# Adaptive layer-norm sums of a Conformer/mLSTM block: half the step rate over the q products, the rest over the wk products, and another PSUM bank

## The chip, the cores and the metric

The kernel runs on one core of a Trainium2 chip. The metric is the device time of one execution in microseconds (us), lower is better. The kernel before takes 1817.89 us, the median of three runs (1816.94 to 1818.36). A change of this kernel of less than about 0.2% (3.6 us) cannot be told from no change.

Five engines work side by side, each through its own list of instructions in the order of the list: TensorE (PE in the profile; its weight loads are listed as PEld), VectorE (DVE), ScalarE (ACT), GpSimd (POOL) and SyncE (SP). SP issues nearly all the loads from memory here, also in the order of its list. An instruction that waits holds up everything behind it on its engine.

## The reference

The block is two layers over 256 latent tokens (model width 1024) with 256 context tokens ahead of them. Layer 0 mixes tokens by a convolution, layer 1 by a bidirectional mLSTM with 4 heads of width 512; each is followed by an MLP with squared ReLU. All is float32. Each sub-layer is modulated by six vectors, which a matrix product of the conditioning vector gives:

```
def adaln(cvec, w, b):
    return jnp.split(jax.nn.silu(cvec) @ w + b, 6, axis=-1)
...
for i in range(DEPTH):
    sh1, sc1, g1, sh2, sc2, g2 = adaln(c[:, None, :], ada_w[i], ada_b[i])
    csh1, csc1, cg1, csh2, csc2, cg2 = adaln(c_ctx, ada_w[i], ada_b[i])
    u = modulate(h, sh1, sc1)
    ...
    h = layer_norm(ALPHA * h + g1 * y, ln1_g[i], ln1_b[i])
    h = layer_norm(ALPHA * h + g2 * sq_relu_mlp(modulate(h, sh2, sc2), ...), ...)
```

`ada_w[i]` is a 1024 x 6144 matrix, and there are only two rows to multiply with it: `c` and `c_ctx`. In the mLSTM the queries are `xc @ w_q` and the keys `xc @ w_k`. The kernel does not make the keys for the scores; it multiplies the queries with `w_k` first and then with `xc`.

## The kernel before

**Matrix products.** Every float32 operand is split into a high and a low part (`wh` and `wl` for weights), and one product is three matmuls (lines 177, 180 and 181). Weights come in 1 MB loads into a tile `raw` (line 150, three buffers); ACT casts 128x1024 of it to `wh` (line 154), DVE subtracts to get `wl` (line 155), with four buffers each. Results go to PSUM banks: a kind `mm` with three banks, `ln` with two, `cv` with two and `fl` with one. `psum()` without a name takes the next `mm` bank.

**adaLN of layer 1.** Part of this product is not done by TensorE. The class `AdaV` does it in steps: a step loads 128x512 of `ada_w` into a tile `ar` (line 353; one buffer, so the next load waits until DVE has read this one) and DVE multiplies it with one column of `c` and `c_ctx` and adds to two accumulators `L` (line 357 for the first step of eight, line 359 for the other seven). After eight steps the accumulators hold, for 512 outputs, one partial sum per partition. `rows` adds these over the partitions by two matmuls with a matrix of ones (line 372) into a PSUM bank, and ACT copies the result to a tile `F` (line 374). After two such halves (one in the last unit) `end` transposes `F` by four matmuls (line 381), and DVE adds the bias (line 382).

There are five units of this in two lists. `ada_n1` runs inside the MLP of layer 0, one step per block of 128 outputs. `ada_n2` has three units, 40 steps: 16 steps run during the last half of the v product, and the other 24 in what follows. Its steps are called by the loops of the other products:

- `queries(h)` makes the queries of head `h`: eight pieces of 24 matmuls (128x256), each with 128x1024 of `wq`, and one step after each piece.
- `pair(p)` makes the queries of two heads, then runs over the 16 row blocks `m` of `wk`: for each, 24 matmuls of 128x272 (12 per head) into `mm` banks, the split of the result into `rr`, and 12 matmuls of 128x512 into four score accumulators, which are the two `ln` banks, one `cv` bank and the `fl` bank.

Pair 0 (heads 0 and 1) therefore takes 16 steps in its two `queries`, the whole second unit, and pair 1 eight steps in the first of its two, the third unit.

**What sets the order.** The program is written in the order above, and a scheduler then sets each engine's list by its own estimates. It may put an instruction later or earlier than written, as long as the data allow it; on the chip the list is fixed. Buffers are given by turn: a tile that takes the next `mm` bank shifts the bank of all `mm` tiles behind it, and must wait for the bank's last reader.

Of the kernel before, what the change touches and what calls it, by code (L numbers as in the profile page):

```python
# [21 lines left out]
C = 256  # L22
# [50 lines left out]
def hybrid_kernel(ctx: ExitStack, tc: tile.TileContext, xT, vecs_d, wdw_d, ada0_w, ada_w, wg_d, pw1a, pw1, pw2, w1_0, w2_0,  # L73
# [12 lines left out]
    def nm(s):  # L86
        uid[0] += 1
        return f"{s}_{uid[0]}"
# [3 lines left out]
    def tmp(tag, dt=F32):  # L92
        return tp.tile([P, T], dt, tag=tag, name=nm(tag), bufs={"E": 4, "S": 2, "L": 2, "F": 1}[tag])
# [8 lines left out]
    def psum(tag="mm"):  # L102
        return pp.tile([P, 512], F32, tag=tag, name=nm(tag), bufs={"mm": 3, "ln": 2, "fl": 1, "cv": 2}[tag])
# [44 lines left out]
    def raw_load(src):  # L148
        raw = wp.tile([P, 2048], F32, tag="raw", name=nm("raw"), bufs=3)
        nc.sync.dma_start(raw[:, :src.shape[-1]], src)  # L150
        return raw
# [8 lines left out]
    def split_w(src, make=None):  # L160
        n = src.shape[-1]
        if make is not None:
            his, los = [], []
            for i in range(0, n, T):
                his.append(make(F32R))
                los.append(make(F32R))
                split(his[-1], los[-1], src[:, i:i + T])
            return his, los
        hi = wp.tile([P, 1024], F32R, tag="wh", name=nm("wh"), bufs=NW)[:, :n]
        lo = wp.tile([P, 1024], F32R, tag="wl", name=nm("wl"), bufs=NW)[:, :n]  # L170
        anchors.append(split(hi, lo, src))
        return hi, lo
# [3 lines left out]
    def mm3(ps, wh, wl, xh, xl, start, stop):  # L176
        a = nc.tensor.matmul(ps, wh, xh, start=start, stop=False)  # L177
        if pin[0]:
            tc.keep_in_program_order(a)
        nc.tensor.matmul(ps, wh, xl, start=False, stop=False)  # L180
        nc.tensor.matmul(ps, wl, xh, start=False, stop=stop)  # L181

    def kcol(w, kt):
        if isinstance(w[0], list):
            w, kt = (w[0][kt // 4], w[1][kt // 4]), kt % 4
        return w[0][:, kt * P:(kt + 1) * P], w[1][:, kt * P:(kt + 1) * P]
# [5 lines left out]
    def gemm_steps(w_ap, groups, rhs, n, epi, ko=0, pre=None):  # L192


        if isinstance(rhs, dict):
            parts = [(LO, rhs[0]), (HI, rhs[1])]
        else:
            parts = [(slice(0, n), rhs)]
        kh_n = len(parts[0][1]) // 8
        groups = list(groups)  # L200
        pre = pre or {}
        raws = {}
        if ko:
            ws, pss = [], []
            for m in range(ko):
                g = groups[m // 2]
                if m not in pre:
                    if g not in raws:
                        raws[g] = raw_load(w_ap[g, 0])
                    pre[m] = split_w(raws[g][:, (m % 2) * 1024:(m % 2 + 1) * 1024])  # L210
                ws.append(pre[m])
                pss.append(psum("mm" if m < 3 else "cv")[:, :n])
            for kt in range(8):
                for m in range(ko):
                    mm3(pss[m], *kcol(ws[m], kt), *rhs[kt], kt == 0, kt == 7)
            for m in range(ko):
                epi(m, pss[m])
        for gi, g in enumerate(groups):
            if 2 * gi + 1 < ko:
                continue  # L220
            ms = [m for m in (0, 1) if 2 * gi + m >= ko]
            pss = {m: psum()[:, :n] for m in ms}
            for kh in range(kh_n):
                raw = raws.get(g)
                for m in ms:
                    w = pre.get((g, kh, m))
                    if w is None:
                        if raw is None:
                            raw = raw_load(w_ap[g, kh])
                        w = split_w(raw[:, m * 1024:(m + 1) * 1024])  # L230
                    for sl, r in parts:
                        for kt in range(8):
                            mm3(pss[m][:, sl], *kcol(w, kt), *r[kh * 8 + kt], kh == 0 and kt == 0,
                                kh == kh_n - 1 and kt == 7)
                    if kh == kh_n - 1:
                        epi(gi * 2 + m, pss[m])
                    yield
# [103 lines left out]
    class AdaV:  # L341
# [22 lines left out]
                self.end()  # L364

        def rows(self, n):
            ps = psum("fl")
            if n == 0:
                self.sb = tmp("F")
            for s in range(2):  # L370
                j = 32 * (2 * n + s)
                nc.tensor.matmul(ps[j:j + 32, :], ones[:, 0:32], self.acc[s], start=True, stop=True,  # L372
                                 tile_position=(0, j))
            nc.scalar.copy(self.sb[64 * n:64 * n + 64], ps[64 * n:64 * n + 64])

        def end(self):
            nu, o = self.nu, _OFF[f"ada_b{self.l}"][0] + 4 * self.u0
            r = 64 * nu
            tr = psum("fl")[:, 0:4 * r]
            for b in range(4):  # L380
                nc.tensor.transpose(tr[:, b * r:(b + 1) * r], self.sb[:r, b * P:(b + 1) * P], ident[:r, :r])
            nc.vector.tensor_tensor(
                ada[self.l][:, 4 * self.u0:4 * (self.u0 + nu), :].rearrange("p (v b) s -> p b v s", b=4),
                tr.rearrange("p (b v s r) -> p b v s r", b=4, v=nu, s=2)[:, :, :, :, 0],
                vecs[:, o:o + 4 * nu].rearrange("p (v b o) -> p b v o", b=4, o=1).broadcast_to([P, 4, nu, 2]), op=ALU.add)
# [302 lines left out]
    for h_ in range(2):  # L688
        wd = F()[:NTAP, :]
        nc.sync.dma_start(wd, wdw_d[0:NTAP, h_ * 512:(h_ + 1) * 512])  # L690
        for t, w_ in ((Hc, WC), (Hs, WS)):
            ps = psum("ln")
# [253 lines left out]
    ada_g2, ada_n1, ada_n2 = Ada(0, 10, 2), AdaVs(1, 0, 4), AdaVs(1, 4, 8 - Z.fill)  # L946
# [131 lines left out]
    def flush():  # L1078
        while late:
            late.pop(0)()  # L1080
# [26 lines left out]
    preq = {(0, 0, m): split_w(rx[:, m * 1024:(m + 1) * 1024]) for m in (0, 1)}  # L1107
# [5 lines left out]
    xcl = [(h_[:, HI], l_[:, HI]) for h_, l_ in xcs]  # L1113
# [5 lines left out]
    def queries(h):  # L1119
        qq = []  # L1120

        def q_epi(m, ps):
            if m < 2:
                flush()
            t = qd.tile([P, 2, QW], F32R, tag="qq", name=nm("qq"), bufs=8)
            split(t[:, 0, :C], t[:, 1, :C], ps)
            split(t[:, 0, C:], t[:, 1, C:], rk[:, 4 * h + m, :])
            qq.append((t[:, 0, :], t[:, 1, :]))

        for _ in gemm_steps(wq, range(2 * h, 2 * h + 2), xcl, C, q_epi, pre=preq):  # L1130
            ada_n2.step()
        return qq

    def pair(p):
        qq = [queries(2 * p + i) for i in range(2)]
        flush()
        acc = [psum(t) for t in ("ln", "ln", "cv", "fl")]
        todo = []

        def scores(n):  # L1140
            while len(todo) > n:
                m, r = todo.pop(0)
                for b in range(4):
                    mm3(acc[b], xcs[m][0][:, b * P:(b + 1) * P], xcs[m][1][:, b * P:(b + 1) * P], *r, m == 0, m == ET - 1)

        def end():
            scores(0)
            for b in range(4):
                t = X()
                nc.scalar.mul(t, acc[b], DH ** -0.5)  # L1150
                for i in range(2):
                    S[2 * p + i, b] = t[:, i * C:(i + 1) * C]

        for m in range(ET):
            if m % 2 == 0:
                raw = raw_load(wk[p, m // 2])
                ws = [split_w(raw[:, i * 1024:(i + 1) * 1024]) for i in range(2)]
            r = RR(F32R), RR(F32R)
            for i in range(2):
                ps = psum()[:, :QW]  # L1160
                for kt in range(4):
                    mm3(ps, *kcol(ws[i], m % 2 * 4 + kt), *qq[i][kt], kt == 0, kt == 3)
                split(r[0][:, i * C:(i + 1) * C], r[1][:, i * C:(i + 1) * C], ps[:, :C])
                nc.vector.tensor_tensor(wgp[1][:, m, 0:16], wgp[1][:, m, 0:16], ps[:, C:], op=ALU.add)
            if p == 1 and m % 4 == 2:
                rx = raw_load(xc_dr[m // 4].rearrange("p b c -> p (b c)"))
            scores(0)
            todo.append((m, r))
            if p == 1 and m % 4 == 3:
                for j in range(4):  # L1170
                    gate_acc(j, wgp[1][:, m - 3 + j, :], rx[:, j * T:(j + 1) * T], last=m == ET - 1)
        if p == 0:
            late.append(end)
        else:
            end()
# [89 lines left out]
    for p in range(2):  # L1265
        pair(p)
# [282 lines left out]
```

## Time and profile before

| | |
|---|---|
| median of three runs | 1817.89 us |
| the profiled execution | 1820.06 us, of which the profile's span is 1818.3 us |
| busy in the span: PE, PEld, DVE, ACT | 96%, 83%, 61%, 42% |
| TensorE idle in the span (1818.3 - 1749.5) | 68.8 us |
| mean granted TensorE clock | 0.982 |
| loaded from memory | 278 MB, 162 GB/s over the span |

A row of the page's list of groups gives an engine, an operation, its tiles, how often it ran, the busy time, the mean of one in ns, and the idle time just before with what ended it. The view of waits lists who waited for whom in us. The chain of waits follows the last instruction back, at each step to what released it. A timeline row gives start, length, engine, line, tiles and, in brackets, the idle time before it. TensorE's matmuls overlap: 128x256 shows 0.28 us but starts every 0.12 us.

### The profile page before, as it was taken

What the parts mean: (1) busy time and instruction counts of PE and PEld (TensorE: products, weight loads), DVE (VectorE), ACT (ScalarE), POOL (GpSimd) and SP (SyncE); (2) the same over time, 40 slices, a digit from 0 to 9 for tenths busy, and PEclk for the clock granted to TensorE, in tenths of its full rate; (3) what the DMA queues carried; (4) which work ended last, traced back from release to release, by engine and by line L of the source; (5) the groups of instructions that cost most, each with busy time, mean ns of one, the idle gap of its engine ahead of it and who ended that gap; (6) DMA issues with size and microseconds to landing.
All of it is one profiled execution on the core that took longest, in us unless ns stands there. A gap on an engine that the chain in (4) does not pass through costs nothing.

```text
span 1818.3 us, 28103 instructions
## 1 busy us (share of the span) xinstructions
PE 1749.5 (96%) x11410; PEld 1518.2 (83%) x11410; DVE 1111.2 (61%) x2071; ACT 764.6 (42%) x1212; POOL 8.4 (0%) x60
## 2 busy tenths in 40 slices
PE   8999999999999999999999699999999999979996
PEld 5564998888889999876879599988999999859996
DVE  5456996566446978731347453523777667876666
ACT  4311753223233656522335223423858645434443
POOL 0000000000000000000000000000000000000000
PEclk9999999999999999999999799999999999989998
DMA  9424416334322375677547332443535345455551
GB/s 346 151 104 149 158 57 226 129 129 157 112 96 93 108 246 183 190 267 248 186 155 252 141 126 101 163 139 116 186 125 195 122 169 202 163 206 189 186 186 47
DMA packets 67250, 295.65 MB, mean 163 GB/s; under 512 B 6770, under 2 KB 22642, under 8 KB 36144
## 3 DMA queue, kind: packets, MB, share of 16 engines
q1 hardware_dynamic: 49456, 279.16, 44.1%
q10 hardware_dynamic: 17664, 14.69, 2.4%
q8 instruction: 90, 1.47, 0.3%
q14 instruction: 40, 0.33, 0.1%
HBM read 278.09 MB, written 15.73 MB: 162 GB/s over the span
## 4 chain that ended last, share of the span: by engine, by line
PE 88%; DVE 5%; ACT 3%; DMA 2%; issue 1%; SPq 0%; DVEq 0%; ACTq 0%
PE mm L177 25%; PE mm L181 25%; PE mm L180 25%; DVE wl L155 1%; DMA raw<-ada_w 1%; PE fl L291 1%; PE fl L718 1%; PE cv L787 1%; DMA ar<-ada_w 1%; PE ln L177 1%; ACT wh L154 1%; PE ln L181 1%; PE ln L180 1%; PE mm L762 1%; PE fl L372 1%
## 5 line engine op out<-in xcount | busy, mean ns | idle before, releaser
L155 DVE TENSOR_TENSOR wl<-raw,wh 128x1024 fp32r<-128x1024 f32 x354 | 431.0, 1222 | 323.9 <-ACT wh L154 321.1
L154 ACT CAST wh<-raw 128x1024 fp32r<-128x1024 f32 x354 | 368.6, 1050 | 613.4 <-PE mm L180 529.5
L180 PE MATMUL mm<-u,wh 128*128 128x256 f32 (+1 forms) x1400 | 448.2, 320 | 0.0
L177 PE MATMUL mm<-u,wh 128*128 128x256 f32 (+1 forms) x1272 | 398.7, 315 | 7.4 <-ACT u L1456 2.1
L181 PE MATMUL mm<-u,wl 128*128 128x256 f32 (+1 forms) x1272 | 396.9, 313 | 1.1 <-DVE wl L155 1.1
L180 PEld LDWEIGHTS mm<-u,wh 128*128 128x128 f32 x1400 | 268.4, 192 | 19.5 <-issue 1.6
L177 PEld LDWEIGHTS mm<-u,wh 128*128 128x128 f32 x1272 | 243.6, 192 | 30.4 <-ACT wh L154 7.4
L181 PEld LDWEIGHTS mm<-u,wl 128*128 128x128 f32 x1272 | 244.4, 192 | 16.6 <-DVE wl L155 2.3
L177 PE MATMUL mm<-hid,wh 128*128 128x256 f32 (+1 forms) x512 | 166.2, 325 | 0.0
L181 PE MATMUL mm<-hid,wl 128*128 128x256 f32 (+1 forms) x512 | 165.3, 323 | 0.0
L180 PE MATMUL mm<-hid,wh 128*128 128x256 f32 (+1 forms) x512 | 165.3, 323 | 0.0
L177 PE MATMUL mm<-xl,wh 128*128 128x256 f32 x512 | 147.8, 289 | 1.0 <-ACT wh L154 0.8
L180 PE MATMUL mm<-xl,wh 128*128 128x256 f32 x512 | 146.7, 287 | 0.6 <-DVE xl L155 0.6
L181 PE MATMUL mm<-xl,wl 128*128 128x256 f32 x512 | 146.4, 287 | 0.2 <-DVE wl L155 0.2
L359 DVE SCALAR_TENSOR_TENSOR L<-ar,cs,L 128x512 f32<-128x512 f32 x126 | 90.0, 748 | 68.0 <-DMA ar<-ada_w 68.0
L177 PEld LDWEIGHTS mm<-hid,wh 128*128 128x128 f32 x512 | 97.4, 190 | 9.5 <-ACT wh L154 1.7
L181 PEld LDWEIGHTS mm<-hid,wl 128*128 128x128 f32 x512 | 97.4, 190 | 7.6
L180 PEld LDWEIGHTS mm<-hid,wh 128*128 128x128 f32 x512 | 97.4, 190 | 7.6 <-issue 0.2
L177 PE MATMUL mm<-xm,wh 128*128 128x512 f32 x256 | 102.9, 402 | 0.0
L177 PEld LDWEIGHTS mm<-xl,wh 128*128 128x128 f32 x512 | 99.3, 194 | 3.8 <-issue 1.7
L180 PEld LDWEIGHTS mm<-xl,wh 128*128 128x128 f32 x512 | 99.3, 194 | 1.7 <-DVE xl L155 0.8
L181 PE MATMUL mm<-xm,wl 128*128 128x512 f32 x256 | 100.3, 392 | 0.0
(417 smaller groups left out, 3013.6 us busy)
## 6 DMA issues: line engine op xcount, KB each, us to landing
raw<-w SPq DMA_DIRECT2D x64, 1024.0 KB, 4.9
raw<-wo SPq DMA_DIRECT2D x32, 1024.0 KB, 4.9
raw<-ada_w SPq DMA_DIRECT2D x30, 1024.0 KB, 4.9
ar<-ada_w SPq DMA_DIRECT2D x72, 256.0 KB, 2.8
raw<-wv SPq DMA_DIRECT2D x16, 1024.0 KB, 5.6
raw<-wqT SPq DMA_DIRECT2D x16, 1024.0 KB, 5.3
raw<-wq SPq DMA_DIRECT2D x16, 1024.0 KB, 5.4
raw<-wk SPq DMA_DIRECT2D x16, 1024.0 KB, 4.8
```

The costliest lines, as they stand in the source:

```text
L154: c = nc.scalar.copy(hi, src)
L155: nc.vector.tensor_tensor(lo, src, hi.bitcast(F32), op=ALU.subtract)
L177: a = nc.tensor.matmul(ps, wh, xh, start=start, stop=False)
L180: nc.tensor.matmul(ps, wh, xl, start=False, stop=False)
L181: nc.tensor.matmul(ps, wl, xh, start=False, stop=stop)
L291: a = nc.tensor.matmul(ps[32 * j:32 * j + 32], cs[:, kt, 14 - 2 * v:46 - 2 * v], blocks[kt], start=first and kt < 4, stop=last and kt >= 4 ...
L359: nc.vector.scalar_tensor_tensor(a, w, c, a, op0=ALU.mult, op1=ALU.add)
L372: nc.tensor.matmul(ps[j:j + 32, :], ones[:, 0:32], self.acc[s], start=True, stop=True, tile_position=(0, j))
L718: nc.tensor.matmul(wqs[0][32 * j:32 * j + 32, :], wgp[0][:, kt, :], raw[:, j * 512:(j + 1) * 512], start=kt == 0, stop=kt == ET - 1, tile_ ...
L762: nc.tensor.matmul(xfs[b], fm, A[0:fm.shape[0], t, sl], start=i == 0, stop=i == len(w_) - 1)
L787: return nc.tensor.matmul(o[r:r + 64, :], g_[:, r:r + 64], ps_[b][i], start=i == 0, stop=i == 1, tile_position=(0, r))
```

## The change

Three edits. `rows` and `end` take the next `mm` bank instead of the `fl` bank; this holds for all five units, also those in the MLP. `queries` calls a step after every second piece instead of every piece. And the loop over `wk` calls a step at every odd `m`.

```
         def rows(self, n):
-            ps = psum("fl")
+            ps = psum()
...
         def end(self):
...
-            tr = psum("fl")[:, 0:4 * r]
+            tr = psum()[:, 0:4 * r]
...
-        for _ in gemm_steps(wq, range(2 * h, 2 * h + 2), xcl, C, q_epi, pre=preq):
-            ada_n2.step()
+        for i, _ in enumerate(gemm_steps(wq, range(2 * h, 2 * h + 2), xcl, C, q_epi, pre=preq)):
+            if i % 2:
+                ada_n2.step()
...
             if p == 1 and m % 4 == 2:
                 rx = raw_load(xc_dr[m // 4].rearrange("p b c -> p (b c)"))
+            if m % 2:
+                ada_n2.step()
             scores(0)
```

The 24 steps are now: four in each of `queries(0)` and `queries(1)` (first half of the second unit), eight in the `wk` loop of pair 0 (its second half), and four in each of `queries(2)` and `queries(3)` (third unit). The `wk` loop of pair 1 finds none left.

**SP's list in the `wk` loop of pair 0.** `ar` are the loads of the steps, `raw<-wk` the weights. Before:

```order
L150 DMA raw_9663<-wk 128x2048
L353 DMA ar_9003<-ada_w 128x512
L353 DMA ar_9039<-ada_w 128x512
L353 DMA ar_9071<-ada_w 128x512
L353 DMA ar_9110<-ada_w 128x512
L353 DMA ar_9147<-ada_w 128x512
L353 DMA ar_10003<-ada_w 128x512
L353 DMA ar_10035<-ada_w 128x512
L150 DMA raw_9765<-wk 128x2048
```

And with the change:

```order
L150 DMA raw_9641<-wk 128x2048
L353 DMA ar_9519<-ada_w 128x512
L353 DMA ar_9625<-ada_w 128x512
L150 DMA raw_9747<-wk 128x2048
L353 DMA ar_9731<-ada_w 128x512
L353 DMA ar_9837<-ada_w 128x512
L150 DMA raw_9853<-wk 128x2048
L353 DMA ar_9943<-ada_w 128x512
L353 DMA ar_10031<-ada_w 128x512
L150 DMA raw_9971<-wq 128x2048
```

Seven step loads stood in a row; now there are two at most between two weight loads.

**TensorE's list around the second unit's last sum.** `mm<-qq,wh` are the products with `wk`, `rr` the score matmuls. Before, in the third row block (`m` = 2):

```order
L180 MATMUL mm_9313<-qq_8847,wh_9257 128x272
L181 MATMUL mm_9313<-qq_8847,wl_9258 128x272
L372 MATMUL fl_9151<-L_8893,ones 32x512
L372 MATMUL fl_9151<-L_8894,ones 32x512
L381 MATMUL fl_9155<-ident,F_8857 128x128 x4
L177 MATMUL fl_9164<-rr_9175,u_7973 128x512
L180 MATMUL fl_9164<-rr_9176,u_7973 128x512
```

With the change, behind the last row block's products (`m` = 15):

```order
L180 MATMUL mm_9927<-qq_9103,wh_9859 128x272
L181 MATMUL mm_9927<-qq_9103,wl_9860 128x272
L372 MATMUL mm_9947<-L_9199,ones 32x512
L372 MATMUL mm_9947<-L_9200,ones 32x512
L177 MATMUL ln_9117<-rr_9863,xc_8544 128x512
L180 MATMUL ln_9117<-rr_9864,xc_8544 128x512
L181 MATMUL ln_9117<-rr_9863,xc_8545 128x512
L177 MATMUL ln_9118<-rr_9863,xc_8544 128x512
L180 MATMUL ln_9118<-rr_9864,xc_8544 128x512
L181 MATMUL ln_9118<-rr_9863,xc_8545 128x512
L177 MATMUL cv_9119<-rr_9863,xc_8544 128x512
L180 MATMUL cv_9119<-rr_9864,xc_8544 128x512
```

The sum went from the third of the 16 row blocks to the last, its transposes (L381) stand behind eight score matmuls instead of directly behind the sum, and nothing of `AdaV` stands ahead of the first use of the `fl` bank by the scores. The first half's sum now stands directly behind the last product of `queries(1)`, ahead of the first product with `wk`; before, it stood early in the last piece but two.

**TensorE's list in the MLP of layer 0, end of the first product of its second quarter.** `u` is the input of the first product, `hid` that of the second:

```order
 L181 MATMUL mm_3333<-u_1907,wl_3377 128x512
-L372 MATMUL fl_3416<-L_3118,ones 32x512
-L372 MATMUL fl_3416<-L_3119,ones 32x512
+L372 MATMUL mm_3416<-L_3118,ones 32x512
+L372 MATMUL mm_3416<-L_3119,ones 32x512
+L381 MATMUL mm_3420<-ident,F_3074 128x128 x4
 L177 MATMUL mm_3432<-hid_3114,wh_3428 128x512
 L180 MATMUL mm_3432<-hid_3115,wh_3428 128x512
```

The transposes came nine matmuls behind the sum and now follow it directly; the same happens once more in the third quarter, and at the third unit's sum, which now stands at the end of `queries(3)`, where eight matmuls stood between before.

## The prediction

> **What bounds the kernel now.** I read the page first, then the list of waits of TensorE over the whole span, then the chain and the timeline where the longest wait lies.
>
> ```profile
> PE 1749.5 (96%) x11410; PEld 1518.2 (83%) x11410; DVE 1111.2 (61%) x2071; ACT 764.6 (42%) x1212; POOL 8.4 (0%) x60
> PE   8999999999999999999999699999999999979996
> PEclk9999999999999999999999799999999999989998
> ```
>
> TensorE is busy 96% of the span and the only engine near its limit, so a change of VectorE's work counts only where TensorE waits for it. Both the busy row and the clock row have one dent, in the slice at about 1018 to 1045 us. Who was waited for, longest first:
>
> ```profile
> PE fl L372 <- DVE L L359: 17.0, 1, 17.0
> PE fl L291 <- DMA raw<-ada_w: 10.2, 6, 6.6
> PE fl L299 <- DVE F L331: 3.4, 1, 3.4
> ```
>
> A sum (L372) waits once, 17.0 us, for VectorE's accumulation (L359). That is the dent. The other eight sums hardly wait. The chain of waits through it, and TensorE's timeline (the number in brackets is idle time):
>
> ```profile
> 1017.57 1.32 DVE L L359 x2
> 1018.92 4.41 DMA ar<-ada_w
> ...
> 1036.10 1.43 DVE L L359 x2
> 1037.55 2.61 DMA ar<-ada_w
> 1040.25 0.77 DVE L L359
> 1041.06 2.59 PE fl L372 x4
> 1043.66 0.59 ACT F L374
> 1050.22 0.23 PE ln L180
> 1148.03 0.98 PE fl L372 x4
> ```
> ```profile
> 1023.73 0.29 PE L181 MATMUL mm<-qq,wl 128*128 128x272 f32 x1
> 1041.06 2.57 PE L372 MATMUL fl<-L,ones 128*32 128x512 f32 x4 [17.04 <-DVE L L359]
> 1044.30 1.11 PE L381 MATMUL fl<-ident,F 128*128 128x128 f32 x4 [0.67 <-ACT F L374]
> 1045.68 0.79 PE L177 MATMUL fl<-rr,u 128*128 128x512 f32 x1 [0.27 <-DVE ada L382]
> 1048.55 0.29 PE L177 MATMUL mm<-qq,wh 128*128 128x272 f32 x1
> ```
>
> With one `ar` buffer the steps run in series: 1.43 us of accumulation, then 2.61 us of load, so 4.04 us a step and more (4.41 us for the load that shares the memory with a weight load). TensorE's need is given by the windows (columns: busy PE with its count, PEld, DVE, ACT, POOL, then granted clock, DMA share, GB/s):
>
> ```profile
> 980.00:990.00 10.00, 10.00 (x85) 10.00 (x85) 7.46 (x12) 3.90 (x8) 0.00 (x0) 1.00 0.66 205
> 1030.00:1040.00 10.00, 0.00 (x0) 0.00 (x0) 2.83 (x4) 0.00 (x0) 0.00 (x0) 0.50 0.24 79
> 1060.00:1080.00 20.00, 20.00 (x125) 18.16 (x124) 13.34 (x28) 6.60 (x12) 0.00 (x0) 1.00 0.45 150
> ```
>
> In the query stretch 85 matmuls start in 10 us, so a piece of 24 takes 2.8 us. Before asks for a step per piece: 2.8 us against the 4.04 that a step takes. Sixteen steps fall behind by 16 x 1.2 = about 20 us, and the last sum pays it, three row blocks into `wk`: 17 us of wait on what ran in the meantime.
>
> **The change part by part.**
>
> *Term A, the wait removed.* The sum of the second half moves from row block 2 of `wk` to row block 15. A row block has 36 matmuls; at 125 in 20 us that is 5.8 us. Eight steps now have 16 blocks, 93 us, and need 8 x 4.04 = 32 us. The first half's steps have two pieces, 5.6 us, each, above 4.04; were every load as slow as the 4.41, a step of 5.84 would fall behind by 0.2, under 2 us in eight, and term B shows that there is more room. So both sums find their accumulators ready. From the last matmul before the stall to the first product after it, 1048.55 - 1023.73 = 24.8 us passed. What ran there costs at full clock: that last matmul 0.1, the sum 0.98 (the row at 1148.03), four transposes about 0.4, eight score matmuls at 0.23, 1.85; together 3.3. Gain 21.5 us. This counts 17.0 of wait, 0.9 of two small ones, and the rest slow clock: the sum took 2.59 us instead of 0.98. Bounds: 17.0 if only the wait goes, 21.5 if all does. I take 21.5, because the slow matmuls start with the wait's end and the clock is 0.50 in the window of the wait.
>
> The Trainium skill, page "TensorE: Matmul & The Clock Gate", section Part 1, says that TensorE falls to half clock after about 3.4 us of idleness and needs about 3.4 us of work to come back. The 0.50 of the window agrees. By that rule the waits of about 1.2 us that I add below cost no clock; had each cost what the long one did, 7.49 us from 1041.06 to 1048.55 less 3.2 of work and 0.94 of waits, 3.3 us, the sum would end 10 us higher, near 1809.
>
> *Term B, the first half's sum.* It stood at 999.2 and ran as its data came:
>
> ```profile
> 999.21 1.61 PE fl L372 x4
> 998.31 1.41 DVE L359 SCALAR_TENSOR_TENSOR L<-ar,cs,L 128x512 f32<-128x512 f32 x2
> 1009.01 0.29 PE L177 MATMUL mm<-qq,wh 128*128 128x272 f32 x1
> ```
>
> Its accumulation ended at 999.72. It now stands ahead of the first product with `wk`, which began at 1009.01, some 7 us later. So 1.61 falls to 0.98: gain 0.6 (0 to 0.7).
>
> *Term C, the MLP.* The bank moves, the counts do not. In two places the transposes now follow the sum directly and must wait for ACT's copy. Before, nine matmuls covered it:
>
> ```profile
> 380.49 1.05 PE L372 MATMUL fl<-L,ones 128*32 128x512 f32 x4
> 381.47 0.50 PE L177 MATMUL mm<-hid,wh 128*128 128x512 f32 x1
> 381.32 0.59 ACT L900 ACTIVATE E<-mm 128x512 f32<-128x512 f32 x1
> 381.94 0.59 ACT L374 COPY F<-fl 64x512 f32<-64x512 f32 x1
> ```
>
> TensorE is done with the sum at 381.47; the copy, behind the relu (L900), ends at 382.53, and the transposes can begin at about 382.6. Loss 1.15 us, twice: 2.3. Bounds: 0 if the scheduler's new place is hidden by a wait that is there anyway, 4.4 if a weight cast of 1.05 us stands ahead of the copy each time.
>
> *Term D, the third unit's sum*, now at the end of `queries(3)`. The nearest rows are those of its old place at the end of `queries(2)`, where ACT and VectorE have the same list:
>
> ```profile
> 1147.96 1.05 PE L372 MATMUL fl<-L,ones 128*32 128x512 f32 x4
> 1149.16 0.58 ACT L374 COPY F<-fl 64x512 f32<-64x512 f32 x1
> 1150.17 0.42 DVE L155 TENSOR_TENSOR qq<-mm,qq 128x256 fp32r<-128x256 f32 x1
> ```
>
> The sum ends at 1148.94, the copy at 1149.74, so the transposes wait 0.8 us. Sum and transposes take two of the three `mm` banks, so the next product gets the bank of the query just made, which VectorE frees at 1150.59. Without these waits it could begin at 1148.94 + 0.4 = 1149.3. Loss 1.3 (0.8 to 2.5, with one more 1.2 us `wl` ahead of the split).
>
> *At nothing:* the other seven sums and the second unit's transposes. A sum takes the bank next in turn, whose reader was done a piece (2.8 us, 5.5 in the MLP) ago, and eight score matmuls, 8 x 0.23 = 1.85 us, cover the copy of 0.59 at row block 15; uncovered, it would cost about 1. Also VectorE's steps in the `wk` loop: before has steps of the third unit there at 1060 to 1080 us, with VectorE at 13.3 of 20 and TensorE at its full 125 matmuls. SP's list loses a row of seven waiting loads ahead of a weight load:
>
> ```profile
> raw<-wk SPq DMA_DIRECT2D x16, 1024.0 KB, 4.8
> ```
>
> Weights land 4.8 us after issue and one load serves two row blocks, 11.6 us, with three buffers, so that row held up nobody and its end gives nothing.
>
> Sum: 21.5 + 0.6 - 2.3 - 1.3 = 18.5 us. The profiled execution took 1820.06, and its changed twin should take 1801.6 (span 1799.8). The median lies 2.2 lower: 1817.89 - 18.5 = **1799.4 us**.
>
> **The rivals.**
>
> *R1: the `mm` banks pay at every sum.* Nine sums and five sets of transposes now take turns with the products; if each of the 14 held TensorE by 1.15 us, it would lose 16.1 instead of 3.6: 1817.9 - 22.1 + 16.1 = 1811.9. For it: three places do wait by my own count. Against it: at the others the bank's reader is long done.
> The Trainium skill, "Perfetto Trace Analysis", sections Matmuls and Matmul Optimizations, speaks for R1: independent groups should rotate through different banks, and all eight should be in use; the change leaves `fl` empty in these stretches and crowds three banks. That no wait of TensorE on a bank's reader stands high in the list above speaks against it.
>
> *R2: another sum is late instead.* The third unit has eight steps in the 16 pieces of `queries(2)` and `queries(3)`, 5.6 us a step. If each load queues behind a 1 MB weight load, a step takes longer than that. The tile's view gives the span of landings:
>
> ```profile
> DMA to landing us min/median/max: 2.6/2.8/6.6
> ```
>
> At the worst, 6.6 + 1.43 = 8.0 us, eight steps fall 19 us behind: 1818, no change. Against it: the median of 2.8, and the list before had the same one-load-a-weight-load pattern in its first two queries with TensorE full (85 in 10 us).
>
> *R3, slower: VectorE's list blocks the weights.* An accumulation that waits for its load holds the `wl` behind it, which TensorE needs. A step's stretch of 5.6 us holds 1.43 of step, two `wl` of 1.22 and one query split of 0.42, 4.3 us; a full wait for the load of 2.6 makes it 6.9, 1.3 us too long. Over 24 steps that is 31 us: 1830. It decides from 18.5/24 = 0.77 us a step. What VectorE waited there before:
>
> ```profile
> L155 DVE TENSOR_TENSOR wl<-raw,wh 128x1024 fp32r<-128x1024 f32 x44 | 53.6, 1223 | 45.3 <-ACT wh L154 44.1 <-PE fl L372 1.2
> 988.60 1.42 DVE L359 SCALAR_TENSOR_TENSOR L<-ar,cs,L 128x512 f32<-128x512 f32 x2 [0.73 <-DMA ar<-ada_w]
> 993.05 1.42 DVE L359 SCALAR_TENSOR_TENSOR L<-ar,cs,L 128x512 f32<-128x512 f32 x2 [0.68 <-DMA ar<-ada_w]
> ```
>
> 0.7 us of wait makes 5.0 us, which fits into 5.6; and the `wl` sits idle for ACT's cast, so it has room. That speaks against R3.
>
> *That the change does not do what it says* is ruled out by the lists: the sum stands at row block 15, and the list on the chip is fixed.
>
> **How the numbers follow.** Forecast 0.84, R1 0.08, R2 0.04, R3 0.04. The forecast's own range: all small waits hidden, 1817.9 - 22.1 = 1795.8; at their upper ends (4.4 and 2.5), 1802.7; with 17.0 only for the stall and mid losses, 1803.9. With a little for the run to run spread, 1795 to 1805; that leaves out the rivals, 0.16. What can be told from no change is 0.2%, 3.6 us. Faster: forecast and R1, 0.92. Same: R2, 0.04. Slower: R3, 0.04.
>
> **What would show it.** In the changed profile the wait of L372 for L359 should be gone from the list, the clock row should have no dent near 1030 us, and the windows of pair 0's `wk` loop should hold 125 matmuls per 20 us from its start to its end. A wait of L381 for ACT's L374 should appear, about 1.1 us in each of two places near 382 and 472, and 0.8 near the end of the fourth query product. The forecast is wrong if L372 waits for L359 anywhere by more than 2 us, if TensorE waits for `wl` in the query stretch, or if waits on `mm` banks sum to more than 8 us.

## The result and the profile after

The changed kernel takes 1797.66 us, the median of four runs (1797.3 to 1800.17), against 1818.12 us before (1816.94 to 1819.11) on the same chip: 20.5 us less, a ratio of 0.9891 with a 95% interval of 0.9874 to 0.9908. The forecast was 1799.4, with 1795 to 1805 as its range. The profiled execution took 1797.44 us, with a span of 1795.7.

From the page of the changed kernel, the busy times and the rows of TensorE and its clock in 40 slices:

```profile
PE 1743.1 (97%) x11410; PEld 1513.9 (84%) x11410; DVE 1111.0 (62%) x2071; ACT 762.7 (42%) x1212; POOL 8.4 (0%) x60
PE   8999999999999999999999999999999999889996
PEclk9999999999999999999999999999999999989998
```

VectorE does the same work to 0.2 us (1111.0 after 1111.2). The dent at 1018 to 1045 us is gone from both rows. TensorE's waits, longest first:

```profile
PE fl L291 <- DMA raw<-ada_w: 13.0, 8, 6.4
PE mm L381 <- ACT F L374: 2.8, 3, 1.0
PE mm L177 <- ACT og L154: 2.6, 2, 2.3
```

The wait of a sum (L372) for an accumulation (L359), 17.0 us before, is not in the list at all. In its place stands a new one, transposes (L381) waiting for ACT's copy (L374), 2.8 us in three places. The windows of the `wk` loop of pair 0 show TensorE full and its clock at 1.00:

```profile
1030.00:1040.00 10.00, 10.00 (x63) 9.08 (x62) 5.32 (x11) 3.38 (x6) 0.00 (x0) 1.00 0.38 147
1040.00:1060.00 20.00, 20.00 (x128) 18.28 (x128) 8.55 (x21) 4.55 (x9) 0.00 (x0) 1.00 0.39 132
1060.00:1080.00 20.00, 20.00 (x124) 18.11 (x124) 8.38 (x20) 6.33 (x12) 0.00 (x0) 1.00 0.32 106
```

The two new waits that the prediction priced, in TensorE's timeline, one in the MLP and one at the third unit's sum:

```profile
380.65 0.66 PE L381 MATMUL mm<-ident,F 128*128 128x128 f32 x4 [1.03 <-ACT F L374]
1149.13 1.05 PE L372 MATMUL mm<-L,ones 128*32 128x512 f32 x4
1150.96 0.46 PE L381 MATMUL mm<-ident,F 64*128 64x64 f32 x4 [0.78 <-ACT F L374]
1151.35 0.39 PE L177 MATMUL mm<-qq,wh 128*128 128x272 f32 x1
```

Between two traces one can put the time where it belongs by taking the distance between two instructions that both have. For this I use the first sum in the MLP, the first matmul of the v product that reads `x`, the first and the last product with `wk`, and the issue of the first store to the output. "Again" is a second profiled execution of the same kernel.

| stretch (us) | before | before again | changed | changed again |
|---|---|---|---|---|
| start to the first sum of the MLP | 335.8 | 334.2 | 333.8 | 333.3 |
| to the v product | 416.6 | 416.6 | 418.7 | 418.7 |
| to the first product with `wk` | 256.6 | 256.6 | 255.9 | 255.9 |
| to the last product with `wk` | 254.4 | 255.8 | 233.7 | 233.6 |
| to the first store to the output | 546.7 | 545.7 | 545.4 | 545.4 |

The change costs 2.0 us in the MLP (418.65 less 416.63 before rounding), wins 0.7 up to the first product with `wk` and 20.7 to 22.2 from there to the last: 20.1 us on the mean of the two executions before, against 20.5 by the medians. The first row and the last show what is chance; in the fourth, too, the two executions of the kernel before differ by 1.4 us.

What the change did not touch is the rate of the steps in the query stretch. VectorE does 22 accumulations from 960 to 1030 us, as many as before (the row of the kernel before is shown with the two buffers below):

```profile
L359 DVE SCALAR_TENSOR_TENSOR L<-ar,cs,L 128x512 f32<-128x512 f32 x22 | 15.5, 748 | 6.5 <-DMA ar<-ada_w 6.5
```

The eight steps of the second unit's first half start from 959.28 to 998.31 us before and from 959.38 to 998.50 after, one every 5.6 us in both, and the unit's accumulators are complete at 1041.7 before and 1047.2 after. What moved is the unit's last sum: TensorE came to it at 1024.0 and now comes to it at 1095.9.

### The profile page after: what moved, and what is told of

It reads as the page before. It is cut to its first block, busy times and chain, and to the rows that moved or that the text cites. A ratio compares the mean times of both kernels' runs of the same rounds, so it can differ in the third digit from the quotient of the medians.

```text
span 1795.7 us, 28106 instructions
## 1 busy us (share of the span) xinstructions
PE 1743.1 (97%) x11410; PEld 1513.9 (84%) x11410; DVE 1111.0 (62%) x2071; ACT 762.7 (42%) x1212; POOL 8.4 (0%) x60
## 4 chain that ended last, share of the span: by engine, by line
PE 88%; DVE 5%; ACT 3%; DMA 2%; issue 1%; SPq 0%; ACTq 0%; DVEq 0%
PE mm L177 25%; PE mm L181 25%; PE mm L180 24%; DVE wl L155 2%; DMA raw<-ada_w 1%; PE fl L291 1%; ACT wh L154 1%; PE fl L718 1%; PE cv L787 1%; PE ln L177 1%; PE ln L181 1%; PE ln L180 1%; PE mm L762 1%; PE cv L181 1%; PE cv L180 1%
## 5 line engine op out<-in xcount | busy, mean ns | idle before, releaser
L180 PEld LDWEIGHTS mm<-u,wh 128*128 128x128 f32 x1400 | 268.3, 192 | 18.5 <-DVE mv L522 0.8
L359 DVE SCALAR_TENSOR_TENSOR L<-ar,cs,L 128x512 f32<-128x512 f32 x126 | 90.0, 748 | 56.8 <-DMA ar<-ada_w 56.7
## 6 DMA issues: line engine op xcount, KB each, us to landing
raw<-w SPq DMA_DIRECT2D x64, 1024.0 KB, 4.9
raw<-wo SPq DMA_DIRECT2D x32, 1024.0 KB, 4.8
raw<-ada_w SPq DMA_DIRECT2D x30, 1024.0 KB, 5.0
raw<-wv SPq DMA_DIRECT2D x16, 1024.0 KB, 5.4
raw<-wqT SPq DMA_DIRECT2D x16, 1024.0 KB, 5.5
raw<-wq SPq DMA_DIRECT2D x16, 1024.0 KB, 5.3
raw<-wk SPq DMA_DIRECT2D x16, 1024.0 KB, 4.9
```

The source lines that it names most:

```text
L359: nc.vector.scalar_tensor_tensor(a, w, c, a, op0=ALU.mult, op1=ALU.add)
```

## The experiments

My theory: a step is a load and an accumulation in series because of its one buffer, 4.04 us or more; a query piece of 2.8 us is too short for it, two pieces (5.6 us) are enough; and what the bank costs is three short waits. The rivals were that the bank is what held TensorE, that VectorE itself is too slow for a step a piece, and that the difference is partly chance.

**The bank alone.**

```
         def rows(self, n):
-            ps = psum("fl")
+            ps = psum()
...
-            tr = psum("fl")[:, 0:4 * r]
+            tr = psum()[:, 0:4 * r]
```

> Only the bank of the sums and transposes is changed; the steps are called as in the kernel before, one after every query piece. Theory (a step takes about 4.04 us with its one load buffer, and a query piece gives it 2.8): the gain comes from the calls, not from the bank. In this list the two sums of the second unit stand at the ends of queries(0) and queries(1), where their accumulators are late by 8 x 1.2 = about 10 us each, and the third unit's sum at the end of queries(2) by about as much: the waits of L372 for L359 sum to 20 to 30 us instead of 17, plus 2 us in the MLP, so 1818 to 1832 us, not faster than before. Rival (the bank is what held TensorE, because the scores need the fl bank): 1800 us or less, as the whole change.

Measured: 1831.94 us against 1818.64 before, a ratio of 1.0076 (1.0061 to 1.0091). TensorE's waits in it:

```profile
PE mm L372 <- DVE L L359: 27.0, 2, 14.1
PE fl L291 <- DMA raw<-ada_w: 10.0, 6, 6.3
PE mm L381 <- ACT F L374: 3.5, 4, 1.0
```

The bank without the calls makes the kernel slower, by 13 us. With an `mm` bank the scheduler puts the sums at the ends of the two query products, earlier than before, and two of them wait 27.0 us in all (14.1 and 12.9) where one waited 17.0. The third unit's sum, which the expectation had waiting too, did not wait. Each of the two waits is longer than the 10 us expected, because a step took more than 4.04 us: the steps of the first half start 5.5 us apart, from 960.69 to 998.97. The third unit's steps ran early in the `wk` loop and were done 77 us ahead of their sum. So the gain is not the bank's alone. The calls without any `mm` bank were not run; the next kernel comes closest to it.

**The bank only where it must change.** During the `wk` loop the scores hold the `fl` bank, so the second unit's second sum needs another. All other sums and transposes get `fl` back; the calls stay thinned.

```
-            ps = psum()
+            ps = psum("mm" if (self.l, self.u0, n) == (1, 6, 1) else "fl")
...
-            tr = psum()[:, 0:4 * r]
+            tr = psum("mm" if self.u0 == 6 else "fl")[:, 0:4 * r]
```

> The changed kernel, but only the second unit's second sum and its transposes use an mm bank; all others have the fl bank back, which is free at their places. Theory: terms C and D of the prediction come from the bank alone, 1.0 us at each of two places of the MLP and 1.3 us at the third unit's sum; they go and the rest stays, so 3.3 us less than the changed kernel, about 1794.4, and the waits of L381 for L374 go from the list. Rival (the mm bank costs nothing, the waits only show what would be waited for anyway): the same as the changed kernel, 1797.7 within 1.

Measured: 1795.44 us (1793.8 to 1796.3), a ratio to the kernel before of 0.9873 (0.9858 to 0.9888), against 1798.17 (1796.77 to 1799.45) and 0.9889 (0.9874 to 0.9904) for the changed kernel in the same comparison. That is 2.7 us less by the medians, where the three waits in the profile sum to 2.8. The intervals of the two ratios overlap; what shows the mechanism is the trace. Its list of waits has no L381 any more:

```profile
PE fl L291 <- DMA raw<-ada_w: 14.4, 8, 6.5
PE fl L299 <- DVE F L331: 3.5, 1, 3.5
PE mm L177 <- ACT og L154: 2.6, 2, 2.3
```

and from its first sum of the MLP (334.54) to its v product (751.2) it takes 416.7 us, as the kernel before does, not 418.7.

**The changed kernel again.**

> The changed kernel once more, to see which differences between two executions of the same program are chance. Theory: 1797.7, with the first sum of the MLP anywhere between 333 and 336 us, because the kernel's first 340 us are not touched by the change. Rival (the 1.9 us by which the first sum came earlier and the 1.5 us won behind the second score loop belong to the change): the first sum again at 333.8.

Measured: 1798.17 us. The first sum came at 333.3, the rest is in the table. That first sum alone does not settle it, since both executions of the changed kernel lie at the early end. The further kernels do: every engine has the same list up to there, and the first sum comes at 334.5 (in two), 335.2, 336.6 and, in one, 340.8. So the start varies by itself.

**Two buffers for the step loads, calls and bank as before.** The loads go to the two buffers of a temporary tile, `S`, that nothing else uses in this stretch, instead of the one of `ar`.

```
-            w = adp.tile([P, 512], F32, tag="ar", name=nm("ar"))
+            w = tmp("S") if self.u0 >= 6 else adp.tile([P, 512], F32, tag="ar", name=nm("ar"))
```

> The kernel before (steps after every query piece, fl bank), but the step loads of the second and third unit take turns in two buffers, so that a load runs while the step before is added. Theory (what made the last sum late is that load and accumulation run in series): a step now takes the longer of 2.6 to 2.8 us of load and VectorE's share, 1.43 + 1.22 + about 0.3 = 2.95 us a piece of 2.8, so sixteen steps fall behind by 2 to 3 us instead of 20, and the time is 1798 to 1803. Rival (VectorE itself is too slow for a step a piece, so the calls had to be thinned): the wait of L372 stays above 10 us, 1810 or more.

Measured: 1798.81 us (1794.29 to 1802.76), a ratio of 0.9889 (0.9866 to 0.9912): as much as the whole change wins, with all 16 steps still called one per piece and the `fl` bank kept; the four runs lie 8.5 us apart, so the equality is a coarse one. VectorE's groups in the stretch from 960 to 1030 us, of this kernel and of the kernel before:

```profile
L359 DVE SCALAR_TENSOR_TENSOR L<-S,cs,L 128x512 f32<-128x512 f32 x40 | 28.1, 743 | 7.3 <-DMA S<-ada_w 7.2
L155 DVE TENSOR_TENSOR wl<-raw,wh 128x1024 fp32r<-128x1024 f32 x19 | 22.7, 1215 | 0.0
```
```profile
L155 DVE TENSOR_TENSOR wl<-raw,wh 128x1024 fp32r<-128x1024 f32 x20 | 24.2, 1222 | 8.7 <-ACT wh L154 8.7
L359 DVE SCALAR_TENSOR_TENSOR L<-ar,cs,L 128x512 f32<-128x512 f32 x22 | 15.5, 747 | 10.0 <-DMA ar<-ada_w 10.0
```

The same engine does 40 accumulations in the 70 us where it did 22, and waits less for their loads. The 16 steps of the second unit take 48.4 us (960.08 to 1008.48), 3.0 each, where they took 82.4 (959.28 to 1041.66), 5.1 each. The last sum stands even earlier, at 1010.07, and finds its accumulators ready. VectorE was not too slow; it was kept waiting by the one buffer.

**Each step's load done twice, calls and bank as in the changed kernel.**

```
             nc.sync.dma_start(w, ada_w[self.l, self.u0 + n, kt // 4, :, kt % 4 * 512:kt % 4 * 512 + 512])
+            if self.l == 1 and self.u0 >= 6:
+                nc.sync.dma_start(w, ada_w[self.l, self.u0 + n, kt // 4, :, kt % 4 * 512:kt % 4 * 512 + 512])
```

> The changed kernel, but every step of the second and third unit loads its 256 KB twice into its one buffer, one load after the other; what is computed is the same. Theory (a step is load plus accumulation in series, and half the call rate is enough because 4.04 us fit into 5.6): a step now takes 2.6 + 2.6 + 1.43 = 6.6 us, too long for the 5.6 us that two query pieces give, so the second unit's first sum and the third unit's sum wait again, each for 8 x 1.0 us and whatever the loads lose in the list, less the 7 us of room that the first had: together 5 to 25 us, 1803 to 1823; the second sum of the second unit, with 93 us for 8 x 6.6 = 53, does not wait. Rival (the loads are hidden, only the number of VectorE's instructions counts): 1798 within 2.

Measured: 1836.6 us, a ratio of 1.0095 (1.0067 to 1.0122), some 37 us above the changed kernel by the two ratios (it ran on another chip, with 1820.18 for the kernel before) and 12 above the 25 that I gave as the most. TensorE's waits (two more lines in the program move the sum to line 374 and the accumulation to line 361):

```profile
PE mm L374 <- DVE L L361: 30.7, 2, 18.4
PE fl L291 <- DMA raw<-ada_w: 11.2, 7, 6.6
```

Two sums wait, as expected, and the sign is that of the theory: with the load made longer than the calls allow, the old wait is back, twice. The size was wrong, because a step did not take the 6.6 us expected: seven steps took 66.2 us in the second unit's first half (accumulations from 967.50 to 1033.73), 9.5 each, and 63.6 in the third unit, 9.1 each. In the first half a weight load stands between the two loads of a step in four of these seven steps, and the last step's load stands behind three more weight loads than in the changed kernel. The rest of the loss is in part the clock behind the waits, 0.63 in 1035 to 1042 us and 0.50 in 1192 to 1200.

**The kernel before again.**

> The kernel before once more. Theory: the wait of L372 for L359 is 17 us within 1 again, since it follows from the lists, while the first sum of the MLP may come anywhere between 333 and 337 us and the slow clock behind the second score loop (3.4 us at half speed near 1273 us) may be there or not. Rival (that slow clock belongs to the kernel before): there again, at the same matmul.

Measured: a span of 1817.1 us, and

```profile
PE fl L372 <- DVE L L359: 17.1, 1, 17.1
```

The wait is 17.1 us after 17.0: it comes with the lists, not by chance. The slow clock near 1273 us is not there in this execution, so it does not belong to the kernel before (the last section has the rows).

**Both: the `fl` bank where it is free, and two step buffers.**

> The kernel with the fl bank where it is free, and with two step buffers for the second and third unit. Theory: no sum waits any more in that kernel, so a second buffer finds nothing to hide: 1795.4 within 1. Rival (VectorE's waits for step loads still hold up weights in the query stretch): 1 to 3 us less.

Measured: 1794.96 us (1794.6 to 1796.78), a ratio of 0.9863 (0.984 to 0.9885), where the kernel with the bank alone put right had, on another chip, 1795.44 and 0.9873 (0.9858 to 0.9888). No difference that these runs can tell, as the theory has it: once no sum waits, a second buffer finds little to hide.

## Why the prediction was right, step by step

- **Term A, the wait removed, 21.5 us: right.** From the first to the last product with `wk` the changed kernel is 20.7 to 22.2 us shorter, with the loss of term D inside; with D at its measured 0.8 that makes term A 21.5 to 23.0. Of the bounds 17.0 and 21.5 the upper was the right one: the slow clock behind the wait (0.50 in the window before, 1.00 now) went with it. The reason given, that a step in series does not fit into a piece, is shown by the two buffers, which win the same in another way, and by the doubled load, which brings the wait back. The size of a step was wrong: not 4.04 us, which comes close only in the stall (4.2, seven step loads in a row), but 5.6 in the query stretch, where weight loads stand between them in SP's list. So the sixteen steps were not about 20 us behind but 32.7 (complete at 1041.7, where the products with `wk` began at 1009.0), and two pieces, 5.6 us, left a step no room at all. The forecast did not suffer, because it took the gain from the stall itself and not from this count. The room came from the places of the sums: the first half's accumulators were complete at 999.9 for a sum at 1007.4, the second's at 1047.2 for a sum at 1095.9.
- **Term B, the first half's sum, 0.6: right**, 0.7 measured.
- **Term C, the MLP, 1.15 twice, 2.3: right in place and mechanism, a little too large.** Each wait is 1.03 us, and the stretch is 2.0 us longer; with the `fl` bank back it is as long as before.
- **Term D, the third unit's sum, 1.3: too large.** The copy is waited for as priced (0.78 us, 0.8 given). The second part, 0.5 us for a bank that VectorE frees last, did not come: the next product starts at 1151.35, right behind the transposes, while VectorE's split of the last query runs until 1151.76. I had given the banks out by turn; the product stands in a bank that was free sooner.
- **R1, all sums pay for the bank**, did not happen: three of 14 places wait, the three that were named, and they wait for ACT's copy, which the transposes read, not for a bank. The rule of the Trainium skill that speaks for it ("Perfetto Trace Analysis", section Matmuls: independent groups rotate through different banks) names a cost that the waits of TensorE here do not show: none is for the reader of an `mm` bank. Giving the bank back wins 2.7 us by the medians because the scheduler then puts other matmuls between the sum and its transposes again.
- **R2 and R3** did not happen. The accumulations wait for loads 6.5 us in all in the 70 us of the query stretch, 10.0 before, and no sum is late. The doubled load shows R2 at work: steps of 9.5 and 9.1 us are too long for 5.6.
- **The clock of the short waits.** The window from 380 to 384 us, in which a wait of 1.03 us ends, has a granted clock of 1.00:

```profile
380.00:384.00 4.00, 3.35 (x17) 2.83 (x18) 3.40 (x7) 1.20 (x2) 0.00 (x0) 1.00 0.47 123
```

  The windows around the other two, 470 to 474 and 1148 to 1152 us, have 1.00 as well. So these waits cost only themselves, as the rule of the Trainium skill ("TensorE: Matmul & The Clock Gate", section Part 1) had it; the 10 us that the other case would have cost are not there. The last section has a place that this rule does not cover.

The sum of the terms was 18.5 us; with C at 2.0, D at 0.8 and B at 0.7 it would have been 19.4, which leaves 1.1 us of the 20.5 measured to term A and to chance.

## What to carry to other kernels

When one engine waits for another that is only half busy, look at the buffer between a load and its use before the amount of work: load and use in series set a least time per step. A second buffer makes the steps faster; calling them less often did not here, but it moved the reader of their result down the list, to a place by which the slow steps are done. Take the time of a step from the stretch in which it runs: other loads in the same queue made it 5.6 us here, where the bare sum gave 4.04. A sum moved to a shared bank cost nothing here where other work stood between it and its transposes, and 0.8 to 1.0 us where the scheduler put the two side by side, so keep the private bank wherever it is free. To compare two traces, compare distances between the same instructions: the start of this kernel varied by several us from one execution to the next and had nothing to do with the change.

## What was not expected

TensorE's clock fell to half for some 3.4 us in a place without a long wait. In the kernel before, behind the second score loop, it follows on eight small matmuls and two waits of under 0.7 us; the matmuls of 128x256 then start every 0.21 us until 1276.25, where the normal distance is 0.12:

```profile
1270.52 0.96 PE L1205 MATMUL ln<-foldg,L 128*128 128x16 f32 x8
1271.66 0.50 PE L177 MATMUL mm<-xl,wh 128*128 128x256 f32 x2 [0.18 <-ACT xl L154]
1272.80 0.45 PE L180 MATMUL mm<-xl,wh 128*128 128x256 f32 x1 [0.64 <-DVE xl L155]
1273.05 0.41 PE L181 MATMUL mm<-xl,wl 128*128 128x256 f32 x1
...
1276.25 0.35 PE L181 MATMUL mm<-xl,wl 128*128 128x256 f32 x1
```

The windows show it as a granted clock below 1, in the kernel before and not in its second execution, which has the same lists:

```profile
1272.00:1282.00 10.00, 9.36 (x66) 9.20 (x65) 9.52 (x28) 8.01 (x18) 0.07 (x1) 0.83 0.59 212
```
```profile
1270.00:1280.00 10.00, 9.15 (x72) 8.54 (x71) 9.48 (x31) 8.02 (x21) 1.16 (x3) 1.00 0.60 215
```

So the lists do not decide whether this thin place costs the clock; it differs from one execution to the next, and it is about 1.5 us here. The kernel with two step buffers has it in the same place, and the other seven of the nine profiled executions do not; with so few nothing more follows. The length of a wait does not decide it either: TensorE idled for 0.82 us here (1271 to 1273 us), less than the 1.03 us in the MLP that left the clock at 1.00. That the short waits of the changed kernel cost no clock is therefore what these executions show, and not a bound.
